# The result written with channels on the partitions, and the last norm summed across tiles

## The chip, the cores and the metric

One core of a Trainium2 chip runs the whole program. The metric is device time in microseconds (us) of one execution, the median of several runs. The engines are PE (matrix products, with PEld for its weight loads), DVE (VectorE), ACT (ScalarE), POOL (GpSimd) and SP, which here issues transfers. Each runs its own instructions in order and waits for the others by semaphores.

## What is computed

One layer of an encoder over 2048 tokens of 1024 channels: a mixing block, cross attention, a feed-forward block, and a final norm. The change lies in the end of the feed-forward block and the final norm:

```python
h = h + jnp.square(jax.nn.relu(_rms_norm(h, norm_ff_g[l]) @ ff_w1[l])) @ ff_w2[l]
return _rms_norm(h, final_norm_g)

def _rms_norm(x, g):
    y = xf * lax.rsqrt(jnp.mean(xf * xf, axis=-1, keepdims=True) + EPS)
    return (y * g.astype(jnp.float32)).astype(x.dtype)
```

The mean runs over the 1024 channels of a token, and `g` is one factor per channel. The result has shape (1, 2048, 1024).

## The kernel before

All of the work is float32. A product is made from three matmuls of rounded halves (`mm3`, L293): the high half of each operand (`ah`, `bh`) is a copy that ACT makes, the low half (`al`, `bl`) is the difference, made by DVE or POOL (`halves`, L1289). One `mm3` costs three matmuls: L295 (`bh`, `ah`), L296 (`bl`, `ah`) and L297 (`bh`, `al`).

The second feed-forward product is split by a Strassen-like scheme: seven products i for each of four groups o, in the order 1, 6, 7, 5, 3, 2, 4, with sums of the products in tiles `acc[i, tp]` of 128 channels by 4 by 512 tokens. Channels lie on the partitions, tokens along the row. The loop at L1547 runs over steps s = 0 to 223: (product n, token half tp, k), with 12 matmuls in each step (4 banks m by 3). A product of one half fills four PSUM banks over its four steps, `mm` for tp = 0 and `hy` for tp = 1; after k = 3, DVE adds each bank to `acc` (L1576). In the last group (o = 3, steps 168 to 223) further sums of `acc` tiles follow (`add`, L1540, on DVE or POOL, recorded on L1542), after which a tile is a finished part of h. Steps 192 to 199 are product i = 5, 200 to 207 i = 3, 208 to 215 i = 2 and 216 to 223 i = 4.

`fetch_b` (L1403) loads the activations of a step, three steps ahead, into a ring `wr` of six tiles and makes `bh` on ACT and `bl` on DVE; after s = 199 POOL makes `bl` for every k but 0. `fetch_a` (L1377) prepares the weights of the next product, `al` on POOL; for i = 3, 2 and 4 the weights too come through `wr`.

The final norm is worked in four blocks c of 512 tokens. `turn` (L1506) transposes one 128-token slice of a half tile on PE (four 128x128 transposes with the identity, L1509, into a PSUM bank), squares and sums it on ACT (L1511, `accum_out`, into `ss`) and scales it by the gains, a 128 by 1024 tile `gl`, on DVE (L1512). `finish` (L1514) makes the reciprocal root of the mean square of 512 tokens on DVE in a chain of 128x4 operations (L1517 to L1522 with `rsqrt`, L144 to L156), scales the eight slices (L1529 on ACT, in the last block every other one by L1527 on DVE) and has SP store them (L1533). These pieces wait in a list `outs`; the loop takes one or two from it per step (L1567), which sets the program's order, and what is left when the loop ends follows it. Blocks 1 and 3 are complete after i = 3, blocks 0 and 2 after i = 4, so they come last. A scheduler of the build then sets the order of each engine.

Of the kernel before, what the change touches and what calls it, by code (L numbers as in the profile page):

```python
# [18 lines left out]
L = 2048  # L19
D = 1024  # L20
# [77 lines left out]
class Prog:  # L98
# [1267 lines left out]
    def ffn(self):  # L1366
        nc, tc, a = self.nc, self.tc, self.a
# [5 lines left out]
        prods = [(o, i) for o in range(4) for i in self.ORDER_DOWN]  # L1373
# [25 lines left out]
        def sums_w(k, op=nc.gpsimd.tensor_tensor):  # L1399
            op(self.WD[k, 2], self.WD[k, 1], self.WD[k, 2], ALU.add)  # L1400
            op(self.WD[k, 1], self.WD[k, 0], self.WD[k, 1], ALU.subtract)

        def fetch_b(s, eng=nc.vector):  # L1403
            n, tp, k = down[s]
            o, i = prods[n]
            bq[s] = self.halves(self.raw(hc[tp, i - 1, 4 * o + k]), ("bh", "bl"), 6, eng)

        with tc.tile_pool(name="up", bufs=1) as U:
# [23 lines left out]
            for n, (tp, g, i) in enumerate(steps):  # L1432
                if n < 2:
                    self.load_w1(n)
                if n < 12 and n % 2 == 0:
                    j = self.ORDER_UP[n // 2 + 1]
# [5 lines left out]
                if n + 2 >= len(steps):  # L1442
                    k = n + 2 - len(steps)
# [5 lines left out]
                u, c = us.setdefault(g, {}), cs.setdefault(g, {})  # L1449
# [14 lines left out]
                else:  # L1464
# [5 lines left out]
                    t = [U.tile([128, 512], F32, tag="t", name="t", bufs=4) for _ in range(4)]  # L1470
# [11 lines left out]
        with tc.tile_pool(name="down", bufs=1) as B:  # L1482
            acc, ms = {}, []
            on = [B.tile([128, D], F32, tag="on", name="on", bufs=2) for _ in range(2)]
            for tp in range(2):
                for h in range(2):
                    v = on[tp][:, 512 * h:512 * h + 512]
                    nc.sync.dma_start(out=v, in_=msd[2 * tp + h])
                    ms.append(v)
            for i in (1, 6, 7, 4, 5, 3, 2):  # L1490
                for tp in range(2):
                    acc[i, tp] = B.tile([128, 4, 512], F32, tag="acc", name="acc", bufs=14)
            gl = B.tile([128, D], F32, name="gl")
# [10 lines left out]
            ss = B.tile([128, 4, 2, 4], F32, name="ss")  # L1504

            def turn(c, h, src, dst, t, tag):  # L1506
                pt = self.ps.tile([128, 512], F32, tag=tag, name=tag, bufs=4)
                for k in range(4):
                    nc.tensor.transpose(pt[:, 128 * k:128 * k + 128], src[:, k, 128 * t:128 * t + 128], self.ident)  # L1509
                junk = B.tile([128, 512], F32, tag="junk", name="junk", bufs=1)  # L1510
                nc.scalar.activation(junk, pt, AF.Square, accum_out=ss[:, c, h, t:t + 1])  # L1511
                nc.vector.tensor_tensor(dst[:, t], pt, gl[:, 512 * h:512 * h + 512], ALU.mult)  # L1512

            def finish(c, dst, last):  # L1514
# [7 lines left out]
                nc.vector.tensor_tensor(rv, rv, rb, ALU.mult)  # L1522
                for h in range(2):
                    for t in range(4):
                        v = dst[h][:, t]
                        if last and t % 2:
                            nc.vector.tensor_scalar(v, v, rv[:, t:t + 1], None, ALU.mult)  # L1527
                        else:
                            nc.scalar.mul(v, v, rv[:, t:t + 1])  # L1529
                        if last and t % 2 or t == 3:  # L1530
                            n = 2 if last else 4
                            r0 = 512 * c + 128 * (t + 1 - n)
                            nc.sync.dma_start(  # L1533
                                out=self.out[r0:r0 + 128 * n, 512 * h:512 * h + 512].rearrange("(t p) c -> p t c", p=128),
                                in_=dst[h][:, t + 1 - n:t + 1])

            def turned(c, tp, h, i, j):
                return [lambda tag, t=t: turn(c, h, acc[i, tp], acc[j, tp], t, tag) for t in range(4)]

            def add(i, j, tp, eng):  # L1540
                for m in range(4):
                    eng.tensor_tensor(acc[i, tp][:, m], acc[i, tp][:, m], acc[j, tp][:, m], ALU.add)  # L1542

            early = [(i, tp, k) for i in (7, 4, 3, 2) for tp in range(2) for k in range(4)]
            outs = []
            V, G = nc.vector, nc.gpsimd
            for s, (n, tp, k) in enumerate(down):  # L1547
                o, i = prods[n]
                if n == 0 and tp == 0:
                    sums_w(k, nc.vector.tensor_tensor)  # L1550
                if s + 3 < len(down):
                    fetch_b(s + 3, G if s > 199 and k else V)
                if o < 3 and tp == 0 and i == 2:
                    load_w(o + 1, k)
                if o < 3 and tp == 0 and i == 4:
                    sums_w(k)
                if early and s > 3:
                    residual(*early.pop(0))
# [12 lines left out]
                for m in range(4):  # L1571
                    v = acc[i, tp][:, m]
                    if o == 0 and i in (1, 6, 5):
                        nc.scalar.copy(v, bank[m])
                    else:
                        nc.vector.tensor_tensor(v, bank[m], v, ALU.add)  # L1576
                if o < 3:
                    continue
                if i == 1:
                    add(2, 1, tp, G)  # L1580
                elif i == 6:
                    add(6, 1, tp, V)
                elif i == 7:
                    add(7, 6, tp, V)
                    add(3, 6, tp, G)
                elif i == 5:
                    add(3, 5, tp, V)
                    add(5, 7, tp, G)
                    add(4, 7, tp, G)
                    if tp:  # L1590
                        outs += turned(1, 0, 1, 5, 1)
                elif i == 3:
                    c = 2 * tp + 1
                    if not tp:
                        outs += turned(3, 1, 1, 5, 1)
                    outs += turned(c, tp, 0, 3, 6)
                    outs.append(lambda tag, c=c, d=(acc[6, tp], acc[1, tp]): finish(c, d, False))
                elif i == 2:
                    outs += turned(2 * tp, tp, 0, 2, 7)
# [102 lines left out]
```

## Time and profile before

| what | us |
|---|---|
| median of three runs | 3389.35 (3387.64 to 3394.67) |
| the profiled execution | 3382.57 |
| its span | 3380.9 |
| PE busy in the span | 3200.3 (95%) |
| POOL busy in the span | 1265.5 (37%) |

The profile shows one execution. The span runs from its first to its last instruction, and 1.7 us of the execution lie around it. Rows of the timeline give a start, a duration, engine, line, operation and tiles; busy times of matmuls overlap, since they are pipelined.

### The profile page before, as it was taken

The numbers are of one execution on the slowest core, as the hardware profiler recorded it, in microseconds if no ns is written. First come the engines' busy times: TensorE is split into PE (matmuls) and PEld (weight loads), VectorE is DVE, ScalarE is ACT, GpSimd is POOL, SyncE is SP. The second block draws the span as 40 slices with busy tenths as digits, with TensorE's granted clock in tenths as the row PEclk, the third lists the DMA queues.
The fourth block names the chain that finished last, engine by engine and source line by source line (L and its number), as shares of the span: only waits on it lengthen the run. The fifth ranks groups of instructions, "written<-read, shape, count | busy, mean of one in ns | idle before, by whom it ended". The sixth has DMA issues, their size and how long they took to land.

```text
span 3380.9 us, 46860 instructions
## 1 busy us (share of the span) xinstructions
PE 3200.3 (95%) x15671; PEld 2563.6 (76%) x15671; DVE 2044.1 (60%) x3711; ACT 1491.3 (44%) x2884; POOL 1265.5 (37%) x894
## 2 busy tenths in 40 slices
PE   6999999999999889799999999999999999999997
PEld 5656666677666778688887997888788887888876
DVE  7584324524646755777766554755855577555695
ACT  4344435523454235445444444555655543333335
POOL 2131001200222214534424013876766564434482
PEclk9999999999999999999999999999999999999998
DMA  5356889996999478857557445765654475444434
GB/s 165 116 206 204 278 294 253 283 337 230 242 242 285 154 240 272 270 152 230 182 162 252 147 132 163 226 204 176 209 165 159 146 241 174 128 140 134 134 94 159
DMA packets 480749, 674.55 MB, mean 200 GB/s; under 512 B 41738, under 2 KB 256848, under 8 KB 479484
## 3 DMA queue, kind: packets, MB, share of 16 engines
q1 hardware_dynamic: 478904, 668.70, 62.9%
q0 software_dynamic: 1600, 2.86, 0.4%
q8 instruction: 124, 2.03, 0.3%
q14 instruction: 117, 0.96, 0.1%
q10 hardware_dynamic: 4, 0.00, 0.0%
HBM read 452.23 MB, written 219.18 MB: 199 GB/s over the span
## 4 chain that ended last, share of the span: by engine, by line
PE 55%; DMA 10%; DVE 8%; issue 3%; ACT 2%; POOL 1%; SPq 0%; DVEq 0%; ACTq 0%; POOLq 0%
PE mm L297 11%; PE mm L295 11%; PE mm L296 11%; PE hy L297 5%; PE hy L295 5%; PE hy L296 5%; DVE wl L301 1%; DVE bl L1292 1%; DMA wr<-xs 1%; PE hy L753 1%; DMA rw<-rows 1%; PE hy L720 1%; DMA a<-hd 1%; DMA xn<-in_x_dram 1%; PE hy L1106 1%
## 5 line engine op out<-in xcount | busy, mean ns | idle before, releaser
L301 DVE TENSOR_TENSOR wl<-wn,wh 128x512 fp32r<-128x512 f32 (+1 forms) x352 | 276.0, 816 | 143.4 <-ACT wh L300 143.0
L1292 DVE TENSOR_TENSOR bl<-wr,bh 128x512 fp32r<-128x512 f32 x213 | 236.9, 1118 | 135.5 <-ACT bh L1291 133.3
L1291 ACT CAST ah<-w 128x512 fp32r<-128x512 f32 x284 | 176.2, 622 | 298.6 <-PE hy L296 154.2
L300 ACT CAST wh<-wn 128x512 fp32r<-128x512 f32 (+1 forms) x352 | 202.1, 617 | 216.0 <-PE mm L296 79.0
L295 PE MATMUL mm<-xh,wh 128*128 128x512 f32 x640 | 275.9, 432 | 8.7 <-ACT P L542 7.6
L739 POOL TENSOR_TENSOR b<-b,a 128x512 f32<-128x512 f32 x64 | 88.9, 1389 | 494.4 <-ACT b L737 207.4
L296 PE MATMUL mm<-xl,wh 128*128 128x512 f32 x640 | 266.0, 416 | 0.0
L297 PE MATMUL mm<-xh,wl 128*128 128x512 f32 x640 | 263.5, 412 | 0.2 <-DVE wl L301 0.2
L1292 DVE TENSOR_TENSOR al<-w,ah 128x512 fp32r<-128x512 f32 x236 | 225.6, 957 | 58.9 <-ACT ah L1291 58.9
L1291 ACT CAST bh<-wr 128x512 fp32r<-128x512 f32 x232 | 143.3, 621 | 245.8 <-PE mm L297 177.8
L297 PE MATMUL mm<-bh,al 128*128 128x512 f32 x576 | 224.4, 392 | 7.9 <-DVE al L1292 5.3
L295 PE MATMUL mm<-bh,ah 128*128 128x512 f32 x576 | 226.1, 393 | 0.4 <-DVE u L1417 0.3
L296 PE MATMUL mm<-bl,ah 128*128 128x512 f32 x576 | 224.9, 390 | 0.0
L295 PE MATMUL mm<-act,wh 128*128 128x512 f32 x512 | 201.6, 398 | 5.4 <-ACT wh L300 5.4
L296 PE MATMUL mm<-act,wh 128*128 128x512 f32 x512 | 203.4, 398 | 0.0
L297 PE MATMUL mm<-act,wl 128*128 128x512 f32 x512 | 201.5, 397 | 0.0
L1149 POOL TENSOR_TENSOR ssum<-ssum,sq 128x512 f32<-128x512 f32 x56 | 80.4, 1436 | 270.1 <-ACT sq L1148 267.3
L295 PE MATMUL hy<-bh,ah 128*128 128x512 f32 x448 | 175.2, 391 | 0.0
L296 PE MATMUL hy<-bl,ah 128*128 128x512 f32 x448 | 174.6, 390 | 0.0
L297 PE MATMUL hy<-bh,al 128*128 128x512 f32 x448 | 174.6, 390 | 0.0
L295 PEld LDWEIGHTS mm<-xh,wh 128*128 128x128 f32 x640 | 121.8, 190 | 55.5 <-issue 17.4
L295 PE MATMUL hy<-xh,ah 128*128 128x512 f32 x384 | 152.6, 398 | 9.1 <-ACT ah L1291 8.3
(379 smaller groups left out, 9046.3 us busy)
## 6 DMA issues: line engine op xcount, KB each, us to landing
wr<-hc SPq DMA_DIRECT2D x224, 256.0 KB
w<-in_ff_w_dram SPq DMA_DIRECT2D x176, 256.0 KB
a<-hd SPq DMA_DIRECT2D x128, 256.0 KB
hc<-t SPq DMA_DIRECT2D x128, 256.0 KB
wn<-in_w_in_dram SPq DMA_DIRECT2D x104, 256.0 KB
hc<-q SPq DMA_DIRECT2D x96, 256.0 KB
fs<-a SPq DMA_DIRECT2D x32, 512.0 KB
a<-fs SPq DMA_DIRECT2D x32, 512.0 KB
```

Of the source, the lines that this page charges most:

```text
L295: mm(ps, lh, rh, start=start, stop=False)
L296: mm(ps, lh, rl, start=False, stop=False)
L297: mm(ps, ll, rh, start=False, stop=stop)
L300: self.nc.scalar.copy(hi, src)
L301: self.nc.vector.tensor_tensor(lo, src, hi.bitcast(F32), ALU.subtract)
L720: nc.tensor.matmul(pp, f1[:, p], z[:, jj], start=True, stop=True)
L739: nc.gpsimd.tensor_tensor(xt, xt, hi[:, m], ALU.mult)
L753: nc.tensor.matmul(pp, e2[:, p], r[p][:, jj], start=p == 0, stop=p == 1)
L1106: nc.tensor.transpose(pt[:, 128 * k:128 * k + 128], yn[:, 128 * k:128 * k + 128], self.ident)
L1149: nc.gpsimd.tensor_tensor(ssum, ssum, sq, ALU.add)
L1291: self.nc.scalar.copy(hi, src)
L1292: eng.tensor_tensor(lo, src, hi.bitcast(F32), ALU.subtract)
```

## The change

The output array has shape (1024, 2048), and the host transposes it. The transposes are gone. A finished tile is squared by ACT (L1516), and the squares of a block's eight tiles are added up on POOL, those of the two last tiles of i = 4 on DVE (L1518). Four matmuls with a column of ones (L1529) sum over the partitions, which gives the sum of squares with tokens on the partitions; DVE's chain of 128x4 operations (L1532 to L1536) makes the factor per token, and four multiplications of the identity by it make a diagonal `dg` (L1539). A matmul of ones with `dg` (L1544) spreads the factors over all partitions; ACT copies them from PSUM to `rb` (L1546). Each tile is then multiplied by gain and factor on DVE (L1554); in blocks 0 and 2 the first half was scaled by the gain on ACT before (L1562), and POOL multiplies four, respectively two, of its tiles by `rb` (L1551). A store covers two tiles (L1556). The gains are loaded as 128 by 8. Between `scale_of` and `write` of a block three empty pieces stand in the list; block 0's `write` is held back until that of block 2. The loop takes up to three pieces per step in the last product. All `bl` are made on DVE. L1540 to L1545, L1574 and L1576 of before are L1568 to L1573, L1601 and L1603 now.

```diff
-            gl = B.tile([128, D], F32, name="gl")
-            nc.gpsimd.dma_start(out=gl, in_=a["final_norm_g"].unsqueeze(0).broadcast_to([128, D]))
+            gl = B.tile([128, 8], F32, name="gl")
+            nc.gpsimd.dma_start(out=gl, in_=a["final_norm_g"].rearrange("(k p) -> p k", p=128))
...
+            def power(c, x, eng):
+                fresh = c not in total
...
+                sq = total[c] if fresh else B.tile([128, 512], F32, tag="sq", name="sq", bufs=2)
+                nc.scalar.activation(sq, x, AF.Square)
+                if not fresh:
+                    eng.tensor_tensor(total[c], total[c], sq, ALU.add)
...
+            def scale_of(c, tag):
+                p = bank_of(tag)
+                for t in range(4):
+                    nc.tensor.matmul(p[:, t:t + 1], total[c][:, 128 * t:128 * t + 128], self.ones[:, 0:1], start=True, stop=True)
                 rb = self.rbp[:, 4 * c:4 * c + 4]
                 m = B.tile([128, 4], F32, tag="mo", name="mo", bufs=2)
-                nc.vector.tensor_tensor(m, ss[:, c, 0], ss[:, c, 1], ALU.add)
-                nc.vector.tensor_tensor(m, m, rb, ALU.mult)
+                nc.vector.tensor_tensor(m, p[:, 0:4], rb, ALU.mult)
                 nc.vector.tensor_tensor(m, m, rb, ALU.mult)
                 nc.vector.tensor_scalar(m, m, 1.0 / D, EPS, ALU.mult, ALU.add)
                 rv = self.rsqrt(B, m, "or")
                 nc.vector.tensor_tensor(rv, rv, rb, ALU.mult)
...
+                dg = row("dg")
+                for t in range(4):
+                    nc.vector.tensor_scalar(dg[:, 128 * t:128 * t + 128], self.ident, rv[:, t:t + 1], None, ALU.mult)
+                total[c, "dg"] = dg
+
+            def write(c, halves, tag):
+                p = bank_of(tag)
+                nc.tensor.matmul(p, self.ones, total[c, "dg"], start=True, stop=True)
+                rb = row("rb")
+                nc.scalar.copy(rb, p)
+                dst = self.out.rearrange("(k p) t -> p k t", p=128)[:, :, 512 * c:512 * c + 512]
+                for h, x in enumerate(halves):
+                    for k in range(4):
+                        if c % 2 == 0 and h == 0 and k < 4 - c:
+                            G.tensor_tensor(x[:, k], x[:, k], rb, ALU.mult)
                         else:
+                            g = 1.0 if c % 2 == 0 and h == 0 else gl[:, 4 * h + k:4 * h + k + 1]
+                            V.scalar_tensor_tensor(x[:, k], x[:, k], g, rb, ALU.mult, ALU.mult)
+                        if k % 2:
+                            nc.sync.dma_start(out=dst[:, 4 * h + k - 1:4 * h + k + 1], in_=x[:, k - 1:k + 1])
+
+            def powers(c, x, eng, early=False):
...
+            def ending(c, halves):
+                return [lambda tag: scale_of(c, tag)] + [lambda tag: None] * 3 + [lambda tag: write(c, halves, tag)]
...
-                    fetch_b(s + 3, G if s > 199 and k else V)
+                    fetch_b(s + 3)
...
-                for _ in range(min(len(outs), 2 if len(outs) > 5 else 1)):
+                for _ in range(min(len(outs), 3 if n + 1 == len(prods) else 2 if len(outs) > 5 else 1)):
                     outs.pop(0)("mm" if tp else "hy")
...
                 elif i == 4:
-                    outs += turned(2 * tp, tp, 1, 4, 5)
-                    outs.append(lambda tag, c=2 * tp, d=(acc[7, tp], acc[5, tp]), tp=tp: finish(c, d, tp))
+                    outs += powers(2 * tp, acc[4, tp], V)
+                    end = ending(2 * tp, (acc[2, tp], acc[4, tp]))
+                    outs.append(end[0])
+                    if tp:
+                        outs += [last, end[-1]]
+                    last = end[-1]
...
-    out = nc.dram_tensor("out_0_dram", (L, D), F32, kind="ExternalOutput").ap()
+    out = nc.dram_tensor("out_0_dram", (D, L), F32, kind="ExternalOutput").ap()
...
-    return r.results[0]["out_0_dram"].reshape(1, L, D)
+    return np.ascontiguousarray(r.results[0]["out_0_dram"].T).reshape(1, L, D)
```

More of the change, by code (lines that the diff above doesn't have):

```diff
@@ L1502, in residual, with row, bank_of @@
                     nc.gpsimd.tensor_tensor(v, v, acc[7, tp][:, k], ALU.subtract)
[L1504 to L1514, printed above, removed]
+            V, G = nc.vector, nc.gpsimd
+            total = {}
+            def power(c, x, eng):
+                fresh = c not in total
+                if fresh:
+                    if c % 2 == 1:
+                        pair = B.tile([128, D], F32, tag="on", name="ssum", bufs=2)
+                        total[c], total[c - 1, "room"] = pair[:, 0:512], pair[:, 512:1024]
+                    else:
+                        total[c] = total[c, "room"]
+                sq = total[c] if fresh else B.tile([128, 512], F32, tag="sq", name="sq", bufs=2)
+                nc.scalar.activation(sq, x, AF.Square)
+                if not fresh:
+                    eng.tensor_tensor(total[c], total[c], sq, ALU.add)
+            def row(name):
+                return B.tile([128, 512], F32, tag="rb", name=name, bufs=3)
+            def bank_of(tag):
+                return self.ps.tile([128, 512], F32, tag=tag, name=tag, bufs=4)
+            def scale_of(c, tag):
+                p = bank_of(tag)
+                for t in range(4):
+                    nc.tensor.matmul(p[:, t:t + 1], total[c][:, 128 * t:128 * t + 128], self.ones[:, 0:1], start=True, stop=True)
                 rb = self.rbp[:, 4 * c:4 * c + 4]
                 m = B.tile([128, 4], F32, tag="mo", name="mo", bufs=2)
-                nc.vector.tensor_tensor(m, ss[:, c, 0], ss[:, c, 1], ALU.add)
-                nc.vector.tensor_tensor(m, m, rb, ALU.mult)
+                nc.vector.tensor_tensor(m, p[:, 0:4], rb, ALU.mult)
                 nc.vector.tensor_tensor(m, m, rb, ALU.mult)
@@ L1522, in finish @@
                 nc.vector.tensor_tensor(rv, rv, rb, ALU.mult)
[L1523 to L1527, printed above, removed]
-                        else:
[L1529 to L1535, printed above, removed]
@@ L1540, in add, with one @@
+            def powers(c, x, eng, early=False):
+                def one(k):
+                    power(c, x[:, k], eng)
+                    if early:
+                        nc.scalar.mul(x[:, k], x[:, k], gl[:, k:k + 1])
+                return [lambda tag, k=k: one(k) for k in range(4)]
+            def ending(c, halves):
+                return [lambda tag: scale_of(c, tag)] + [lambda tag: None] * 3 + [lambda tag: write(c, halves, tag)]
             def add(i, j, tp, eng):
@@ L1545, in ffn @@
             outs = []
-            V, G = nc.vector, nc.gpsimd
             for s, (n, tp, k) in enumerate(down):
@@ L1590, in ffn @@
                     if tp:
-                        outs += turned(1, 0, 1, 5, 1)
+                        outs += powers(1, acc[5, 0], G)
                 elif i == 3:
```

10 lines of the change are left out of this document (4 added, 6 removed).

## The prediction

> **What bounds the kernel now.** Times are us from the span's start. I read the page for the whole, then the window table of the end, where all of the change lies.
>
> ```profile
> span 3380.9 us, 46860 instructions
> PE 3200.3 (95%) x15671; PEld 2563.6 (76%) x15671; DVE 2044.1 (60%) x3711; ACT 1491.3 (44%) x2884; POOL 1265.5 (37%) x894
> ...
> 2800.00:2820.00 20.00, 14.66 (x58) 11.67 (x57) 14.77 (x11) 4.69 (x9) 18.12 (x13) 0.83 0.56 186
> 3250.00:3300.00 50.00, 45.88 (x215) 37.06 (x214) 47.02 (x46) 16.91 (x35) 48.99 (x33) 1.00 0.33 101
> 3300.00:3340.00 40.00, 40.00 (x206) 32.88 (x206) 27.72 (x59) 26.56 (x58) 16.81 (x15) 1.00 0.56 184
> 3340.00:3381.00 41.00, 20.02 (x106) 16.50 (x104) 20.78 (x59) 18.51 (x44) 4.80 (x4) 0.77 0.37 135
> ```
>
> After the length the columns are PE, PEld, DVE, ACT, POOL, granted clock, DMA share, GB/s. PE is the bound, but from 3250 to 3300 POOL is busy 49 of 50 and DVE 47 of 50: there the elementwise engines are full, and PE loses 4 us. From 3300 there is slack. The waits of PE from 3218 to 3358, and the chain, name the losses:
>
> ```profile
> PE mm L297 <- POOL al L1292: 2.6, 2, 2.4
> PE hy L1509 <- DVE acc L1576: 1.5, 1, 1.5
> ...
> 3285.36 0.43 PE hy L1509 x4
> 3285.80 0.23 PE mm L295
> ```
>
> A product matmul takes 0.227 (one step of 12: 2.72), four transposes 0.44. PE waits for `al`, the low half of the weights, which POOL makes:
>
> ```profile
> 3275.96 1.71 POOL L1292 TENSOR_TENSOR al<-wr,ah 128x512 fp32r<-128x512 f32 x1
> 3277.63 3.43 POOL L1542 TENSOR_TENSOR acc<-acc 128x512 f32<-128x512 f32 x2
> 3281.02 2.97 POOL L1292 TENSOR_TENSOR al<-wr,ah 128x512 fp32r<-128x512 f32 x2
> ...
> 3294.97 3.79 POOL L1292 TENSOR_TENSOR bl<-wr,bh 128x512 fp32r<-128x512 f32 x3
> ```
>
> The longest wait (2.4) ends with the `al` of step 200, after 3277.6; that of step 201, first of the two in the third row, is done about 3282.7, just as the transposes let PE go: no slack. A POOL operation costs 1.70 while DVE works on SBUF too, and 1.26 when not (last row). The end, by engine timelines and the DMA view of 3364 to 3381 (40 slices):
>
> ```profile
> 3357.23 0.39 PE L297 MATMUL hy<-bh,al 128*128 128x512 f32 x1
> 3364.78 7.45 ACT L1529 ACTIVATE acc<-acc,or_y 128x512 f32<-128x512 f32 x12 [2.69 <-DVE or_y L1522]
> 3367.37 7.44 SPq L1533 DMA_DIRECT2D out_dram<-acc  x6
> GB/s 0 0 0 0 0 0 0 0 0 0 337 390 386 381 381 337 415 386 347 405 366 361 395 376 381 376 386 381 361 381 390 386 386 381 390 371 39 0 0 0
> DMA packets 2144, 4.19 MB, mean 247 GB/s; under 512 B 96, under 2 KB 96, under 8 KB 2144
> ```
>
> The last product ends at E = 3357.6. The first of six stores is issued at E + 9.75; then 4.19 MB flow at a flat 380 GB/s, and the span ends 13.5 later. So the tail is the time to the first store plus a fixed 13.5.
>
> **The change part by part.** *Removed from PE:* 128 transposes, 108 of them before E, in 27 groups of 0.44: 11.9. The 16 at steps 200 to 203 stand where POOL's `al` holds PE, so they buy nothing yet. In the built order of the changed kernel the first square-sum add (L1518) stands on POOL ahead of the `al` of step 201, another ahead of that of step 203. From 3277.63: two adds 3.4, the new add 1.7, `al` 1.7, so PE goes on at 3284.5; the `al` of 202 comes at 3286.1, of 203 at 3289.5, each just in time. Step 204 starts at 3292.2, as now:
>
> ```profile
> 3291.96 0.48 PE L295 MATMUL hy<-bh,ah 128*128 128x512 f32 x1
> ```
>
> From there 240 matmuls at 0.227 are 54.4: without waits E = 3346.6, **−11.0**.
>
> *Added to PE:* three groups of L1529 (four 128x1 matmuls) and two L1544 before E. The same operations stand elsewhere:
>
> ```profile
> 1487.49 0.95 PE L1221 MATMUL hy<-ones,ssum 128*128 128x1 f32 x8
> 1623.29 1.02 PE L1265 MATMUL hy<-ssum,ones 128*128 128x512 f32 x2
> ...
> L197 DVE SCALAR_TENSOR_TENSOR b<-b x8: 674/692/693, 44.2 to 108.8; 128x512 f32<-128x512 f32 x8
> ```
>
> Less overlap I take 0.8 and 0.85: **+4.1** (2.5 to 4.9).
>
> *The new waits.* PE runs in order, and L1529 needs the sums that POOL adds. From 3277.63 to the last add of column block 3 POOL has 27 operations (6 old adds, 7 `al`, 14 square adds). Seven end by 3289.5; the other 20 at 1.5, between 1.26 and 1.70, since DVE is loaded half the time. PE's dates: step 208 reads the 17th operation, an `al` (3304.5), at 3303.5: wait 1.0. Block 1's L1529 stands 165 matmuls before E; PE is there at 3310.2, the 22nd operation ends at 3312.0: 1.8. Block 3's L1529 stands 144 before E; PE arrives at 3317.6, the 27th ends at 3319.5: 1.9. Sum **+4.7**; 0 with POOL at 1.26, +9 at 1.70.
>
> *The round trip.* Right behind it, still 144 before E, stands block 1's L1544, which needs the diagonal `dg` from DVE. Behind its L1532 DVE has, in built order, 21 small operations, four L1603, two `bl` and, among them, block 3's first step, which itself waits for the L1529 just named. Behind it on PE stand the last 144 product matmuls, and for those all of the tail. Prices:
>
> ```profile
> 3328.93 1.31 POOL L1292 TENSOR_TENSOR al<-wr,ah 128x512 fp32r<-128x512 f32 x1 [4.32 <-ACT ah L1291]
> ...
> 3328.93 0.15 DVE L155 SCALAR_TENSOR_TENSOR or_y<-or_t,or_y 128x4 f32<-128x4 f32 x1
> 3329.11 1.15 DVE L153 TENSOR_TENSOR or_t<-or_y 128x4 f32<-128x4 f32 x1
> 3330.29 1.22 DVE L154 SCALAR_TENSOR_TENSOR or_t<-or_t,mo 128x4 f32<-128x4 f32 x1
> ```
>
> A 4-column operation takes 0.2 alone, but 1.2 beside a POOL operation, until whose end it stands. 21 × 0.2 + 4 × 0.6 + 2 × 1.2 is 9.0, and about three blocked operations add 3.5. DVE starts at about 3315.5: L1529 is through at 3312.8, and the `bl` queued before L1532 wait for ACT, whose squares wait for POOL to free one of two `sq` buffers. So `dg` is ready at 3328.1; PE has stood since 3320.3: **+7.8**. Below, only what follows block 3's L1529 counts (2.5); above, DVE starts at 3318 and all is blocked (14).
>
> *The clock.* After the one gap of that length:
>
> ```profile
> 2815.91 0.79 PE L297 MATMUL mm<-bh,al 128*128 128x512 f32 x1 [5.34 <-DVE al L1292]
> 2816.50 0.63 PE L295 MATMUL mm<-bh,ah 128*128 128x512 f32 x1
> 2816.92 0.63 PE L296 MATMUL mm<-bl,ah 128*128 128x512 f32 x1
> ```
>
> the next matmuls come every 0.43 instead of 0.23 and the granted clock of those 20 us is 0.83. Some eight matmuls at 0.2 more are **+1.7**, an estimate from these rows; 0 if the gap stays under the 2.4 of the waits above, where the clock held at 1.00.
>
> *Other edits before E.* DVE takes over 15 `bl` from POOL and gains 16 L1554 and 4 adds; it loses 32 L1512. ACT loses 28 scalings for 8 gains and a few copies.
>
> ```profile
> L1292 DVE TENSOR_TENSOR bl<-wr,bh 128x512 fp32r<-128x512 f32 x32 | 42.3, 1335 | 10.3 <-ACT bh L1291 10.3
> L1576 DVE TENSOR_TENSOR acc<-hy,acc 128x512 f32<-128x512 f32 x28 | 18.1, 678 | 0.7 <-PE hy L297 0.7
> ...
> L1292 POOL TENSOR_TENSOR bl<-wr,bh 128x512 fp32r<-128x512 f32 x15 | 20.2, 1357 | 12.3 <-ACT bh L1291 12.3
> L1509 PE MATMUL mm<-ident,acc 128*128 128x128 f32 x76 | 10.9, 273 | 0.3 <-DVE acc L1512 0.3
> ```
>
> DVE's slack after 3300 (28 of 40 busy) covers most of it. SP queues block 1's four stores, waiting for DVE, ahead of the last four `wr` loads, needed 11 us later; I put **+1.0** for an `al` or a load that is late (0 to 3). The smaller `gl` load on POOL's DMA queue is due 500 us later: nothing. E moves by −11.0 + 4.1 + 4.7 + 7.8 + 1.7 + 1.0 = **+8.3**.
>
> *The tail.* From E − 0.65 DVE has two L1603 and four square adds (about 0.6 each: L1603 is L1576 of now), and of block 0's chain eleven small operations and four for `dg` (0.2 each), 6.7 in all: `dg` at E + 6.0. L1544 and ACT's copy (0.6 each) let POOL start its four L1551 at E + 7.3. DVE is then in block 2's chain with 12 operations left: four of them pass, one per POOL operation of 1.3, to E + 12.5; eight more at 0.2: E + 14.1. Only then come block 0's L1554 (the L197 row prices such an operation at 0.69, less overlap 0.6), and the first pair's store goes at E + 15.4. The 4.19 MB behind it are the same: **+5.7** (from +1.3, if the small operations slip past POOL, to +8).
>
> The sum is +14.0: 3380.9 + 14.0 = 3394.9 of span, with the 1.7 around it 3396.6 where this execution took 3382.57. The median of the runs shown is 3389.35, so the number I give is 3389.35 + 14.0 = **3403**.
>
> **The rivals.** (1) *The waits are covered* (faster). If POOL runs at 1.26, DVE's chain slips through and the first add does not delay `al`, PE is bound by its matmuls alone: −11.9 − 1.5 (the wait at 3282) + 4.1 = −9.3 with an unchanged tail: 3380. It decides at the round trip: `dg` of block 1 by 3320. For it speaks the slack after 3300; against it 49 of 50 on POOL just before.
> (2) *Half of it.* The round trip at its lower end, no clock loss, the tail +3: −11.0 + 4.1 + 2 + 2.5 + 3 = +0.6: 3390.
> (3) *Worse.* POOL at 1.70, all of DVE's chain blocked: some +22: 3411.
> (4) *The transposes are worth more than their spacing.* The group row gives 273 ns as the mean of one; 108 at that are 29.5, not 11.9, and the sum would be −3.6: 3386. Against it stands the chain, where the next matmul starts 0.44 after four of them: the mean includes overlap. The Trainium skill, "TensorE: Matmul & The Clock Gate", Part 4: PE-mode transpose, states about 275 ns in a kernel's context; by it the change would gain that much more. The trace agrees with the duration, not with it as a price.
> (5) *It does not do what it says:* the transposes do go from the built order; nothing for this.
>
> **How the numbers follow.** Forecast (+7 to +17) 0.52, (3) 0.13, (2) 0.20, (1) 0.13, (4) 0.02. A measurement of this kernel tells about 0.2% (6.8 us) from no change. Faster is (1): 0.13. Same is (2) and (4): 0.22. Slower is the rest: 0.65. The range runs from −7, where (1) begins, to the middle of (3): 3382 to 3411; outside lie (1) and half of (3), 0.19.
>
> **What would show it.** Right: PE waits at L1529 and above all at L1544 in the middle of the last product but one, with clock below 1.00 behind it; DVE's 128x4 operations at 1.2 beside POOL; the first store of block 0 about 15 after the last product. Wrong: PE at 100% from 3292 on; or `al` late earlier, so that PE loses more before the squares.

## The result and the profile after

The changed kernel takes 3404.8 us (median of 5 runs, 3398.05 to 3414.03) where the kernel before takes 3389.35 in the same session (5 runs, 3385.59 to 3394.67). The ratio is 1.0048, with a 95% interval of 1.0030 to 1.0065: 15.5 us slower. The forecast was 3403, +14.0.

The page of the profiled execution (3404.8 us, span 3403.1) differs little in its totals: the 88 matmul instructions fewer leave PE's busy time where it was.

```profile
span 3403.1 us, 46680 instructions
PE 3199.8 (94%) x15583; PEld 2555.2 (75%) x15583; DVE 2081.5 (61%) x3736; ACT 1478.6 (43%) x2836; POOL 1295.2 (38%) x905
```

One execution is some us early or late before it reaches the changed stage, so spans alone mislead. I therefore date everything from the start of step 190 (of 224; its first product matmul is the 408th from the end), to which both kernels compute the same. The PE timelines, the kernel before first, then the changed one with its step 190 and its last product:

```profile
3247.02 0.39 PE L295 MATMUL hy<-bh,ah 128*128 128x512 f32 x1
```
```profile
3253.38 0.39 PE L295 MATMUL hy<-bh,ah 128*128 128x512 f32 x1
...
3373.97 0.40 PE L297 MATMUL hy<-bh,al 128*128 128x512 f32 x1
```

The changed kernel's profiled execution was thus 6.4 late before the stage began. From step 190 to the end of the last product (E) pass 110.6 before and 121.0 after (**+10.4**); from E to the end of the span 23.2 and 28.7 (**+5.44**). The sum, +15.8, is close to the difference of the medians (+15.5).

The window table of the end (after the length: PE, PEld, DVE, ACT, POOL, granted clock, DMA share, GB/s):

```profile
3250.00:3300.00 50.00, 46.47 (x193) 36.72 (x192) 48.92 (x45) 16.61 (x29) 46.86 (x29) 0.97 0.34 100
3300.00:3340.00 40.00, 27.91 (x112) 21.21 (x112) 34.32 (x59) 18.68 (x33) 30.85 (x21) 0.85 0.34 105
3340.00:3381.00 41.00, 36.15 (x159) 29.16 (x158) 34.67 (x70) 15.82 (x27) 10.28 (x7) 0.96 0.36 128
```

In 3300 to 3340 PE was busy for all 40 us at clock 1.00; now it is busy for 27.9 at 0.85, while POOL went from 16.8 to 30.9 and DVE from 27.7 to 34.3. (Moved by the 6.4 us, to 3306.4 to 3346.4, the window has the same 27.9 of PE, at 0.83, with 25.3 of POOL and 33.3 of DVE.) The waits of PE (total, count, longest; the `mm` of L1544 and the 3.6 of L1529 are in the tail) name what it stood for, and the timeline shows the worst place:

```profile
PE mm L1544 <- DVE dg L1539: 7.1, 2, 5.8
PE mm L297 <- POOL al L1292: 5.8, 5, 2.4
PE hy L1544 <- DVE dg L1539: 5.3, 1, 5.3
PE mm L1529 <- DVE acc L1603: 3.8, 1, 3.8
PE mm L1529 <- DVE ssum L1518: 3.6, 1, 3.6
```
```profile
3311.80 0.50 PE L297 MATMUL mm<-bh,al 128*128 128x512 f32 x1 [2.30 <-POOL al L1292]
3312.14 0.40 PE L295 MATMUL mm<-bh,ah 128*128 128x512 f32 x1
...
3328.65 1.84 PE L1529 MATMUL mm<-ones,ssum 128*128 128x1 f32 x8 [3.75 <-DVE acc L1603]
3335.80 2.07 PE L1544 MATMUL hy<-dg,ones 128*128 128x512 f32 x2 [5.31 <-DVE dg L1539]
...
3338.52 0.63 PE L297 MATMUL hy<-bh,al 128*128 128x512 f32 x1
3338.95 0.63 PE L295 MATMUL hy<-bh,ah 128*128 128x512 f32 x1
```

Block 3's L1529 and block 1's L1544 follow each other, with 3.75 and 5.31 of standing before them. After them the products come every 0.43 for a while: the granted clock is 0.50 from 3328.3 to 3341.9. What DVE did meanwhile:

```profile
3322.76 0.15 DVE L1532 TENSOR_TENSOR mo<-hy,rbp 128x4 f32<-128x4 f32 x1
3322.95 1.06 DVE L1533 TENSOR_TENSOR mo<-mo,rbp 128x4 f32<-128x4 f32 x1
3324.04 0.17 DVE L1534 TENSOR_SCALAR mo<-mo 128x4 f32<-128x4 f32 x1
3324.24 1.14 DVE L150 TENSOR_SCALAR or_y<-mo 128x4 int32<-128x4 int32 x1
...
3327.82 0.68 DVE L1603 TENSOR_TENSOR acc<-mm,acc 128x512 f32<-128x512 f32 x1
...
3332.86 2.89 DVE L1539 TENSOR_SCALAR dg<-ident,or_y 128x128 f32<-128x128 f32 x4
```

Block 1's chain runs from 3322.8 to 3335.7. Until POOL's adds end at 3326.7 every second of its small operations takes 1.06 to 1.14, and behind that 0.16. The L1603 at 3327.82, which empties a PSUM bank, stands behind the first half of that chain, and it is for this bank that block 3's L1529 waits, not for POOL's sum: the last of POOL's adds for it ends at 3326.7. POOL's timeline, and the group of the square adds from step 190 to E:

```profile
3322.24 4.47 POOL L1518 TENSOR_TENSOR ssum<-ssum,sq 128x512 f32<-128x512 f32 x3
```
```profile
L1518 POOL TENSOR_TENSOR ssum<-ssum,sq 128x512 f32<-128x512 f32 x20 | 29.7, 1491 | 6.4 <-ACT sq L1516 4.6 <-DMA wr<-hc 1.2
```

The tail, by the timelines of three engines:

```profile
3383.10 4.95 DVE L1539 TENSOR_SCALAR dg<-ident,or_y 128x128 f32<-128x128 f32 x4
...
3383.04 4.92 POOL L1551 TENSOR_TENSOR acc<-acc,rb 128x512 f32<-128x512 f32 x4 [25.54 <-ACT rb L1546]
...
3389.40 8.70 SPq L1556 DMA_DIRECT2D out_dram<-acc  x8
```

POOL's four multiplications of block 0 and DVE's four parts of block 2's `dg` advance in step, one for one. The first of the last eight stores goes at E + 15.0 (E + 9.75 before); from it to the end pass 13.65 (13.5 before).

### The profile page after: what moved, and what is told of

It reads as the page before. It is cut to its first block, busy times and chain, and to the rows that moved or that the text cites. A ratio compares the mean times of both kernels' runs of the same rounds, so it can differ in the third digit from the quotient of the medians.

```text
span 3403.1 us, 46680 instructions
## 1 busy us (share of the span) xinstructions
PE 3199.8 (94%) x15583; PEld 2555.2 (75%) x15583; DVE 2081.5 (61%) x3736; ACT 1478.6 (43%) x2836; POOL 1295.2 (38%) x905
## 4 chain that ended last, share of the span: by engine, by line
PE 56%; DMA 9%; DVE 9%; issue 3%; ACT 2%; POOL 1%; SPq 1%; DVEq 0%; ACTq 0%; POOLq 0%
PE mm L297 11%; PE mm L295 11%; PE mm L296 11%; PE hy L297 5%; PE hy L295 5%; PE hy L296 5%; DVE wl L301 1%; DMA a<-hd 1%; PE hy L753 1%; PE hy L1106 1%; PE hy L720 1%; DVE bl L1292 1%; DMA zg<-a 1%; DMA va<-vd 1%; DMA wr<-xs 1%
## 5 line engine op out<-in xcount | busy, mean ns | idle before, releaser
L1292 DVE TENSOR_TENSOR bl<-wr,bh 128x512 fp32r<-128x512 f32 x228 | 258.6, 1141 | 132.4 <-ACT bh L1291 130.4
L297 PE MATMUL mm<-bh,al 128*128 128x512 f32 x576 | 226.4, 394 | 10.4 <-POOL al L1292 5.8
L295 PEld LDWEIGHTS mm<-xh,wh 128*128 128x128 f32 x640 | 122.5, 192 | 56.9 <-issue 17.7
```

Source lines behind the costliest of these rows:

```text
L295: mm(ps, lh, rh, start=start, stop=False)
L297: mm(ps, ll, rh, start=False, stop=stop)
L1292: eng.tensor_tensor(lo, src, hi.bitcast(F32), ALU.subtract)
```

## The experiments

For each kernel I read two stretches from its trace, step 190 to E and E to the end, and compare their sum with the kernel before (133.8):

| kernel | to E | tail | sum, over before | measured ratio (95%) |
|---|---|---|---|---|
| before | 110.6 | 23.2 | 0 | 1 |
| changed | 121.0 | 28.7 | +15.8 | 1.0048 (1.0030 to 1.0065) |
| x1_tailmul | 120.6 | 24.5 | +11.3 | 1.0033 (1.0018 to 1.0047) |
| x2b_write0 | 119.7 | 29.7 | +15.6 | 1.0031 (1.0016 to 1.0046) |
| x4_blpool | 132.4 | 28.5 | +27.0 | 1.0062 (1.0041 to 1.0083) |
| x6_nosum | 112.7 | 23.0 | +1.8 | 1.0012 (1.0000 to 1.0025) |
| y1_before_bl | 113.8 | 23.3 | +3.3 | 1.0007 (0.9992 to 1.0022) |
| y2_before_noT | 111.5 | 16.8 | -5.6 | 0.9995 (0.9978 to 1.0012) |
| x3_late | 124.0 | 27.6 | +17.7 | 1.0041 (1.0017 to 1.0066) |
| x5_addsdve | 119.1 | 29.6 | +14.9 | 1.0043 (1.0029 to 1.0057) |
| x8_apart | 121.3 | 28.3 | +15.7 | 1.0049 (1.0033 to 1.0065) |
| z1_apart_tail | 122.9 | 24.2 | +13.3 | 1.0039 (1.0026 to 1.0051) |
| z2_adds_act | 115.7 | 25.3 | +7.2 | 1.0027 (1.0012 to 1.0041) |
| w1_pesums | 138.0 | 26.3 | +30.4 | 1.0096 (1.0073 to 1.0118) |

Each sum divided by some 3384 lies in the interval beside it, so the two stretches account for the differences of the medians. Each is read from a single execution. Steps 20 to 54, which are the same in all 14 kernels and in which PE stands too, take 97.6 to 99.8 in the 14 traces, so a difference of some 2 us to E can be chance; the four stretches of 34 steps from there to step 190, nearly free of waits, take 92.5 in each of them. My theory: PE loses time because it now reads sums that POOL adds and a diagonal that DVE makes, in a fixed order, and the tail because POOL's multiplications hold up DVE. Rivals: the place of these reads is what is wrong, not the work behind them; or one of the other edits (`bl`, the missing transposes) carries the result.

**x1_tailmul: the tail's POOL multiplications on DVE.**

```diff
-if c % 2 == 0 and h == 0 and k < 4 - c:
-    G.tensor_tensor(x[:, k], x[:, k], rb, ALU.mult)
-else:
+if True:
     g = 1.0 if c % 2 == 0 and h == 0 else gl[:, 4 * h + k:4 * h + k + 1]
```

> POOL's six multiplications at the end (L1551) go to DVE; nothing else changes. E is the end of the last product. Theory: block 2's chain on DVE no longer stands behind POOL's operations, so the four parts of dg take 0.9 instead of 4.95, the first store of block 0 goes at about E + 11 instead of E + 15.0, and the tail is 24 to 25 instead of 28.7; E, counted from the start of step 190, stays at 121 (110.6 in the kernel before). Against the kernel before +10 to +12 us (1.003 to 1.0035). Rival, the eight half-size stores make the tail long: the tail stays at 28 to 29.

The tail is 24.5 in place of 28.7, the way to E as it was. On DVE's timeline in the tail (L1552 is the changed kernel's L1554) the same four operations for `dg` take 0.88 where they took 4.95, with no POOL beside them, and DVE makes all 16 multiplications itself and is still earlier:

```profile
3388.07 0.88 DVE L1539 TENSOR_SCALAR dg<-ident,or_y 128x128 f32<-128x128 f32 x4
3388.86 2.49 DVE L1552 SCALAR_TENSOR_TENSOR acc<-acc,rb 128x512 f32<-128x512 f32 x4
```

So 4.2 of the tail's 5.44 are POOL's help: shown.

**x2b_write0: as x1, and block 0 written ahead of block 2's scale.**

```diff
-outs.append(end[0])
-if tp:
-    outs += [last, end[-1]]
+if tp:
+    outs.append(last)
+outs.append(end[0])
+if tp:
+    outs.append(end[-1])
 last = end[-1]
```

> Block 0's write is put ahead of block 2's scale_of, and POOL's six multiplications go to DVE. Theory: the first store goes when block 0's factor is there, at about E + 9.5, and the tail is limited by 13.5 us of transfers behind it or by block 2's chain, which now comes later: 23 to 27. E, counted from step 190, stays at 121. Rival (half-size stores): the tail stays at 28 to 29.

Block 0's first store goes at E + 10.0, but block 2's first only at E + 21.6, after its chain: the stores have a hole between them, and the tail is 29.7, above both expectations. The profile gives no gain over the changed kernel; the measured ratio, 1.0031, is near x1's. The interval covers both, so this stays open.

**x4_blpool: the 15 `bl` back on POOL, as before the change.**

```diff
-    fetch_b(s + 3)
+    fetch_b(s + 3, G if s > 199 and k else V)
```

> The 15 low halves bl go back from DVE to POOL as in the kernel before; the rest is the changed kernel. Theory (POOL's queue feeds PE's waits): 15 more operations of 1.3 to 1.7 on POOL between step 200 and the end make its sums later; E, counted from step 190, 128 to 140 instead of 121, the whole 1.007 to 1.011 of the kernel before. Rival (DVE is overloaded by the 15 bl it was given, and that delays dg): E falls to 113 to 117 and the whole to 1.000 to 1.003.

E comes 11.4 later than in the changed kernel, with PE waits for POOL's sums of 7.9 and 3.4 and for `bl` of 4.7. The ratio, 1.0062, is a little lower than I expected, and its interval overlaps the changed kernel's. In the trace POOL is the short one: with 15 more operations it makes the sums late, so giving `bl` to DVE was a needed part of the change there; the medians don't tell it apart.

**y1_before_bl: the same edit alone, in the kernel before.**

```diff
-    fetch_b(s + 3, G if s > 199 and k else V)
+    fetch_b(s + 3)
```

> The kernel before with the one edit that gives DVE all bl tiles (15 leave POOL); the transposes and all the rest stay. Theory (this edit helps the changed kernel only because POOL is full of square adds there; in the kernel before POOL and DVE are about equally full): ratio 0.999 to 1.002, last product 109 to 113 us after step 190 starts (110.6 before), tail 22.5 to 24. Rival (this edit alone already costs part of what the change lost, since DVE holds up PE at the row blocks): ratio 1.002 to 1.004, last product 115 or more after step 190.

The way to E is 113.8, a little above what the theory allowed, and the ratio 1.0007, within it: no difference can be measured. The loss doesn't come from this edit.

**x6_nosum: the sums over partitions left out** (L1529 is gone, POOL's adds and L1544 stay).

```diff
-    p = bank_of(tag)
-    for t in range(4):
-        nc.tensor.matmul(p[:, t:t + 1], total[c][:, 128 * t:128 * t + 128], self.ones[:, 0:1], start=True, stop=True)
 ...
-    nc.vector.tensor_tensor(m, p[:, 0:4], rb, ALU.mult)
+    nc.vector.tensor_tensor(m, rb, rb, ALU.mult)
```

> Leaves out the sums over the partitions (L1529): the factors are made from the earlier norm's factors alone, so that dg waits for neither POOL nor PE. The squares and their adds on POOL and DVE are still made, and the four L1544 stay. Theory (the in-order wait of PE for POOL's sums and for DVE's chain costs the middle): PE waits only for al, and E, counted from step 190, is 102 to 106, that is 5 to 9 under the kernel before (110.6); the tail is shorter too, since block 0 can be written before E. Rival (POOL and DVE are simply slowed by the added work, the round trip is not the cause): E stays at 116 to 121.

Of the +15.8, all but 1.8 is gone, both to E (112.7) and in the tail (23.0): reading the sums, and what waits for them, is what costs. E lies between the two expectations, and neither has it. The chain can start early, so L1544 is waited for by no more than 0.4. But E isn't earlier than before, though neither transposes nor sums stand on PE. The waits of PE from step 190 on (L1543 is the changed kernel's L1546):

```profile
PE mm L297 <- POOL al L1292: 5.7, 5, 2.4
PE mm L295 <- ACT rb L1543: 2.5, 1, 2.5
PE hy L296 <- DVE bl L1292: 2.0, 1, 2.0
```

Other work comes late in their place: the halves `al` and `bl` of the operands, and ACT's copy of the factors, on which the first matmul of a product into `mm` waits.

**y2_before_noT: the kernel before with its transposes left out**.

```diff
-    pt = self.ps.tile([128, 512], F32, tag=tag, name=tag, bufs=4)
-    for k in range(4):
-        nc.tensor.transpose(pt[:, 128 * k:128 * k + 128], src[:, k, 128 * t:128 * t + 128], self.ident)
+    pt = src[:, :, 128 * t:128 * t + 128]
 ...
-    nc.vector.tensor_tensor(dst[:, t], pt, gl[:, 512 * h:512 * h + 512], ALU.mult)
+    nc.vector.tensor_tensor(dst[:, t].rearrange("p (a b) -> p a b", a=4), pt, gl[:, 512 * h:512 * h + 512].rearrange("p (a b) -> p a b", a=4), ALU.mult)
```

> The kernel before without the 128 transposes: squares and gains read the slices of acc in SBUF, so the turning is left out and the output is not the reference's; POOL's and DVE's counts of operations stay. Theory (a transpose is worth its spacing of 0.11 us, and those of steps 200 to 203 stand behind POOL's al): last product 97 to 102 us after step 190 (110.6 before), ratio 0.996 to 0.998. Rival 1 (each is worth its mean of 273 ns): last product 81 to 86 after step 190, ratio 0.991 to 0.993. Rival 2 (PE would wait for POOL and DVE anyway, so that the removal buys little): last product 105 to 110 after, ratio 0.998 to 1.000.

Without its 128 transposes the old kernel ends its products 111.5 after step 190, not 110.6, let alone 99.6; only the tail is shorter (16.8: the first of its stores goes 0.4 ahead of E). The measured ratio is 0.9995: no difference can be measured. The first theory falls; rival 2 has the ratio and the waits, and E is 1.5 above its range. Waits of PE after 3218, and a row of the window table:

```profile
PE mm L297 <- POOL al L1292: 4.6, 5, 2.3
PE hy L295 <- ACT bh L1291: 2.7, 1, 2.7
PE mm L295 <- ACT ah L1291: 2.5, 2, 2.0
```
```profile
3292.00:3340.00 48.00, 40.95 (x155) 31.24 (x154) 42.53 (x72) 34.12 (x77) 28.81 (x20) 0.89 0.58 191
```

PE reaches the products sooner and then stands for `al`, `bh` and `ah`; the clock falls to 0.89, where the 48 us from 3292 on were at 1.00 before. The `bh` and `ah` are late because ACT has two groups of eight scalings, 5.01 each, ahead of them with one `bh` between.

The edit does more than leave the transposes out, though: the scaling by the gains, which read a transposed tile in PSUM and `gl` in SBUF, now reads both from SBUF (L1512 before, L1510 in this run; groups from step 190 to E):

```profile
L1512 DVE TENSOR_TENSOR acc<-mm,gl 128x512 f32<-128x512 f32 x14 | 9.6, 688 | 9.3 <-ACT junk L1511 9.2
L1512 DVE TENSOR_TENSOR acc<-hy,gl 128x512 f32<-128x512 f32 x13 | 8.9, 686 | 6.4 <-ACT junk L1511 6.3
```
```profile
L1510 DVE TENSOR_TENSOR acc<-acc,gl 128x512 f32<-128x512 f32 x28 | 29.7, 1118 | 0.1
```

It lasts 1.12 in place of 0.69, which is 11 us more for DVE in this stretch, and POOL's `al` and `bl` last 1.63 and 1.55 in place of 1.40 and 1.36. So the makers of the halves are slower too, and the run doesn't show what the transposes alone are worth. The Trainium skill, "TensorE: Matmul & The Clock Gate", Part 4: PE-mode transpose, gives about 275 ns for one, and the group row's mean of 273 agrees; as the price of 108 of them that would have been 29.5 us here. This run shows no gain of that kind, and in the kernel before four of them in a row take 0.44, not 1.09: what a PE instruction lasts is not what its removal saves.

**x3_late: the round trip apart, 10 empty pieces.**

```diff
-[lambda tag: None] * 3
+[lambda tag: None] * 10
```

> The changed kernel with 10 empty pieces in place of 3 between a block's L1529 and its L1544: block 1's L1544 stands 112 matmuls before the end in place of 144, block 3's L1529 62 in place of 144. Theory (PE stood for the round trip and for what was queued right behind it; 30 to 80 matmuls in between cover it): the waits at block 1's L1544 and block 3's L1529 fall from 5.7 and 4.1 to under 1.5 each, no clock loss behind them, last product 108 to 113 us after step 190 (121.0 in the changed kernel), tail 28 to 31, ratio 0.999 to 1.003. Rival (POOL and DVE are short of capacity, so the wait moves to al, bl or to the tail): last product 116 or more after step 190 or a tail over 33, ratio 1.004 to 1.006.

The waits before block 1's L1544 and block 3's L1529 go from 5.31 and 3.75 to 1.93 and nothing, and step 219 starts 96.0 after step 190 (106.3 in the changed kernel, 95.0 before). But the built order now puts block 0's L1529 48 matmuls before the end, ahead of its sums, and PE stands 8.5 there: 124.0 in all. This settles nothing, as two things moved; hence the next one.

**x8_apart: the round trip apart, and nothing else early.**

```diff
-[lambda tag: None] * 3
+[lambda tag: None] * (7 if c == 1 else 3)
 ...
+if not tp:
+    outs += [lambda tag: None] * 4
 outs.append(end[0])
```

> The changed kernel with 7 empty pieces in place of 3 between block 1's L1529 and L1544, and 4 empty pieces ahead of block 0's L1529, so that (other than in x3_late) nothing new stands early: block 1's L1544 stands 112 matmuls before the end and ahead of block 3's L1529 (108), block 3's L1544 48, block 0's L1529 12. Theory (the order of PE around the round trip costs the 9 us of the waits of 5.3 and 3.75): idle time before these two under 2.5 in sum, last product 110 to 115 us after step 190 (121.0 in the changed kernel, 110.6 before), tail 28 to 30, ratio 1.001 to 1.003. Rival (POOL and DVE lack capacity, another wait takes their place): last product 118 or more after step 190, ratio 1.004 to 1.006.

By its bounds the rival holds: 121.3, no gain. PE's waits:

```profile
PE mm L1544 <- DVE dg L1539: 9.1, 2, 5.8
PE hy L1544 <- DVE dg L1539: 6.4, 1, 6.4
PE mm L297 <- POOL al L1292: 5.7, 5, 2.4
PE mm L1529 <- DVE ssum L1518: 3.6, 1, 3.6
```

Block 1's L1544 (an `mm` here) waits 3.3 in place of 5.3 though it stands 32 matmuls later, block 3's L1529 no longer waits, and block 3's L1544 (`hy`), which did not wait, now waits 6.4. DVE's work behind block 1 (eight L1554 that last 7.45 from 3332.2) comes later too, and block 3's chain behind it. Moving the reads moved the wait. But step 219 starts 97.6 after step 190 here, nearly as before (95.0): as in x3_late, the middle has recovered, and the whole loss comes behind it, at block 3's L1544. No run put that one behind the last product, so a better place isn't excluded.

**x5_addsdve: 14 square adds from POOL to DVE.**

```diff
-outs += powers(1, acc[5, 0], G)
+outs += powers(1, acc[5, 0], V)
 ...
-    outs += powers(3, acc[5, 1], G)
-outs += powers(c, acc[3, tp], G)
+    outs += powers(3, acc[5, 1], V)
+outs += powers(c, acc[3, tp], V)
```

> The changed kernel with the square adds of column blocks 1 and 3 on DVE in place of POOL (14 adds). Theory (POOL's queue is what holds up al of steps 201 and 208 and the sums): al waits of 2.7 and 2.7 fall to under 1 each and L1529 is not waited for; DVE gets 9 to 14 us more work, so L1544 still waits 3 to 6: last product 113 to 118 us after step 190 (121.0), ratio 1.001 to 1.004. Rival (DVE's queue is the bound of the middle stretch): the waits at L1544 or L1529 for DVE grow by as much as POOL's fall: last product 120 or more after step 190, ratio 1.005 to 1.008.

Between the two: 119.1 to E, ratio 1.0043; neither can be told from the changed kernel's 121.0 and 1.0048. The wait for `dg` before E falls from 5.3 to 0.6, those for `al` hardly in sum (5.8 to 5.4); in exchange ACT's `bh` is 7.3 late at step 216.

**z1_apart_tail: x8 and x1 together.**

> x8_apart with the multiplications of the tail all on DVE as in x1_tailmul. Theory (the two effects add): last product 110 to 115 us after step 190, tail 24 to 25.5, together 134 to 140 (133.9 before, 149.7 in the changed kernel), ratio 0.999 to 1.002. Rival (capacity): last product 118 or more after, ratio 1.002 to 1.005.

The tail's gain adds (24.2), the other isn't there to add (122.9): PE waits 8.0 at block 3's L1544. To E the rival holds.

**z2_adds_act: z1, with x5's adds on DVE and `dg` made by ACT.**

```diff
-nc.vector.tensor_scalar(dg[:, 128 * t:128 * t + 128], self.ident, rv[:, t:t + 1], None, ALU.mult)
+nc.scalar.mul(dg[:, 128 * t:128 * t + 128], self.ident, rv[:, t:t + 1])
```

> z1_apart_tail with the square adds of blocks 1 and 3 on DVE as in x5_addsdve, and the four parts of dg made by ACT in place of DVE. Theory (al is then on time, and dg no longer stands behind POOL): last product 107 to 113 us after step 190, tail 23 to 25, ratio 0.997 to 1.001. Rival (ACT's and DVE's queues, as in x5_addsdve where bh came 7.3 late at step 216): last product 115 or more after, ratio 1.001 to 1.004.

The best of the turned versions: 115.7 and 25.3, ratio 1.0027, still slower than before, as the rival had it. PE's waits are spread over all feeders:

```profile
PE mm L297 <- POOL al L1292: 4.1, 4, 2.4
PE mm L295 <- DVE mo L1532: 3.0, 1, 3.0
PE mm L1529 <- DVE ssum L1518: 2.7, 1, 2.7
PE mm L1544 <- ACT dg L1539: 2.6, 1, 2.6
PE hy L1544 <- ACT dg L1539: 1.8, 1, 1.8
```

Taking work off POOL and `dg` off DVE gains 7.2 to E against z1 where moving the reads gained nothing. The two edits weren't run apart.

**w1_pesums: all square adds made by PE itself** (`dg` on ACT and the tail on DVE as in z2).

```diff
-    eng.tensor_tensor(total[c], total[c], sq, ALU.add)
 ...
+for t in range(4):
+    for j, sq in enumerate(sqs):
+        nc.tensor.matmul(p[:, t:t + 1], sq[:, 128 * t:128 * t + 128], self.ones[:, 0:1], start=j == 0, stop=j == 3)
```

> The changed kernel without any square add on POOL or DVE: four squares at a time are summed by PE itself (16 matmuls with one column each, accumulated in PSUM, twice a block, 128 in all); two values of 128x4 are then added. The tail's multiplications are on DVE and dg is made by ACT, as in z2_adds_act; block 1's L1544 stands 130 matmuls before the end, block 3's 60. Theory (the 32 adds of 128x512 on the elementwise engines are what the changed kernel loses; PE gets about as much work back as the transposes were, 6 groups of 16 at 0.11 each, 10.6 us, before the end): last product 108 to 113 us after step 190, tail 23.5 to 26, ratio 0.999 to 1.002. Rival (the round trip to DVE and back is what costs, adds or no adds): PE stands 5 us or more at the two L1544 in sum, last product 115 or more after step 190, ratio 1.002 to 1.005.

Both expectations failed, and the reason is a price that I had wrong. PE waits for no `dg` before E, so the rival's mechanism is not there; but E is 138.0 after step 190. A group of 16 is recorded as 32 passes and takes 3.8, not 1.8:

```profile
3302.64 3.91 PE L1520 MATMUL mm<-ones,sq 128*128 128x1 f32 x32 [1.28 <-DVE acc L1606]
3306.42 0.78 PE L297 MATMUL hy<-bh,al 128*128 128x512 f32 x1
3306.99 0.63 PE L295 MATMUL hy<-bh,ah 128*128 128x512 f32 x1
3307.42 0.63 PE L296 MATMUL hy<-bl,ah 128*128 128x512 f32 x1
```

The row for L1221 in the prediction had said so: `x8` for four matmuls. And the products behind such a group come at 0.43 for some six matmuls. What the kernel does show is that the waits go with the adds: PE stands 4.3 to E (15.6 in the changed kernel), though here ACT makes `dg` as well.

## Why the prediction was right

The total, the sign and the two places were right: +10.4 to E (+8.3 predicted) and +5.44 in the tail (+5.7). Between the 408 product matmuls from step 190 to E lie 407 intervals, 92.4 at 0.227, and the last matmul takes 0.4. From the starts and durations of all matmul records I split the rest into other matmuls, standing, and what is left over (products slower than 0.227): 9.6, 4.1 and 4.1 before; 5.1, 15.6 and 7.5 after. Point by point:

- *The removed transposes, −11.0.* As a count it fits: the other matmuls fell from 9.6 to 5.1, new ones included. As a gain, this is **the step that failed**, as far as the runs show: "From there 240 matmuls at 0.227 are 54.4: without waits E = 3346.6". No kernel without the transposes had E earlier than before, not even x6_nosum (112.7) and y2_before_noT (111.5), which wait for no sums. In y2 PE stands 10.1 for `al`, `ah`, `bh` and `bl` (4.1 before), and the left-over is 8.6 (4.1 before), 5.4 of it in 27 products at half clock, so the 9.6 us of the transposes are filled again. How much of that is the transposes' own slack stays open, since both kernels also load POOL and DVE more: 28.8 and 42.5 of the 48 us from 3292 on in y2, 37.9 and 41.2 in x6_nosum, 24.8 and 32.7 before. That PE would only stand in their place I had seen for steps 200 to 203, and taken the slack after 3300 ("28 of 40 busy") to mean that it ended there. A share of 40 us hides that the halves come in order, behind other work on their engines.
- *Added to PE, +4.1.* Measured 5.1: L1544 takes 2.07 where I took 0.85, since the clock is at half behind the wait.
- *New waits, +4.7.* POOL's rate was right: 1.49 as the mean of 20 adds (1.5 predicted), the last add of block 3 28.7 after the start of step 204 (27.3 predicted). The `al` of step 208 cost 2.3 (1.0), block 1's L1529 0.7 (1.8; the profile puts it down to a load), block 3's 3.75 (1.9). The last one had another cause than I gave, DVE's L1603 in the queue behind block 1's chain. I had named these L1603 only as DVE's load.
- *The round trip, +7.8.* `dg` was ready 37.7 after the start of step 204 (35.9 predicted). PE came 4.4 later than predicted, so 5.3 remained. Right in mechanism and place.
- *Clock, +1.7.* The left-over grew by 3.4, and 18 products at half clock take 4.4 more than at 0.227, so this was mis-sized: half the clock was lost in two places, not one (granted clock 0.50 in 3283.9 to 3287.2 too, behind the first wait for `al`).
- *The tail, +5.7.* First store at E + 15.0 (15.4). The reason given, that DVE passes one operation per POOL operation, is what x1_tailmul shows by taking POOL away; it was the four parts of `dg` that passed so, not the small operations ahead of them. The Trainium skill, "SBUF — State Buffer", section "Who interferes with whom", says that the shared port pair of VectorE and GpSimd is locked for a whole instruction and not divided; 4.95 beside 4.92, against 0.88 alone, agrees.

Rival (1), E earlier by 9.3 if only the waits were covered, was not just unlikely, as I had it: in x6_nosum those for the sums and the round trip are gone, and E is still 2.1 later than before, with other waits in their place. So the forecast was right by terms that hang together otherwise than I thought. I booked a gain of 11.0 and losses of 19.3; the runs show no kernel with that gain, and a loss of 10.4, of which 8.3 hangs on the sums (x6_nosum against the changed kernel). By the split, other matmuls fell by 4.5 (6.9 booked), standing grew by 11.5 (13.5) and the left-over by 3.4 (1.7): errors of both signs that cancel in part, which for the number was luck.

What stays open: why E comes 110.6 to 113.8 after step 190 in four quite different kernels (before, y1, y2, x6), and never earlier. That the making of the operands' halves sets this floor is argued from the waits, in which a different engine is last each time; no run made them cheaper. What the transposes alone are worth was not measured, since y2_before_noT changes the scalings too. Block 3's factors behind the last product were not tried. And z2_adds_act does not tell its two edits apart.

## What to carry to other kernels

Before counting a removed PE instruction as time, ask what arrives next: if the operands' makers (here POOL, DVE and ACT) are just in time, the instruction may only fill a wait. A kernel without it shows its price, if nothing else in that kernel gets dearer. A result that goes from PE to a busy elementwise engine and back waits behind what stands in that engine's queue; in the two orders tried here moving the read moved the wait, and taking work off the queues shortened it. A "helping" engine that shares SBUF access with the helped one can cost more than it carries.

## What the hardware showed that I had not expected

- **The same wait can cost the clock or not.** Step 208 waits 2.30 for `al` in the changed kernel and in x8_apart. In the changed kernel the products go on every 0.23 (rows of 3311.80 above); in x8_apart they come every 0.43 for seven matmuls, and the step takes 6.9 in place of 5.3:

```profile
3305.04 0.72 PE L297 MATMUL mm<-bh,al 128*128 128x512 f32 x1 [2.30 <-POOL al L1292]
3305.55 0.63 PE L295 MATMUL mm<-bh,ah 128*128 128x512 f32 x1
3305.98 0.63 PE L296 MATMUL mm<-bl,ah 128*128 128x512 f32 x1
```

  The Trainium skill, "TensorE: Matmul & The Clock Gate", Part 1, "What's actually happening", says that activity is watched in free-running windows of about 3.4 us, so that the same work can meet them in another phase. That the outcome varies agrees; that it takes an idle window of that length does not quite, at an idle time of 2.30. The same holds at step 200: the first wait for `al`, of 2.4, left the clock at 1.00 before and is followed by 0.50 in the changed kernel. My bound "0 if the gap stays under the 2.4 of the waits above" was no bound.
- **Long groups of one-column matmuls lower the clock without any pause.** In w1_pesums PE is busy all but 1.3 us of the 40 below, and the granted clock is 0.87. The group of 32 passes at 3312.97 follows the products without a wait, and from 3316.3 to 3319.7 the clock is 0.50 all the same. With groups of four transposes (0.44 each, not 3.8) between the products it had been 1.00 in the kernel before.

```profile
3300.00:3340.00 40.00, 38.72 (x199) 33.11 (x198) 21.59 (x42) 16.90 (x31) 6.92 (x5) 0.87 0.31 100
```
